# The row loads of the first eight down units move from the sync engine's queue to GpSimd's

## The chip, the cores and the metric

The kernel runs on one core of a Trainium2 chip. The metric is the time of one execution on the device in microseconds (us). The profile names the engines PE (TensorE, matmuls), PEld (TensorE, weight loads), DVE (VectorE), ACT (ScalarE), POOL (GpSimd) and SP (the sync engine, which here only issues transfers). "SPq" is SP's queue of transfers, and "POOLq" is POOL's.

## The reference

The reference is one decoder block on a sequence of 1024 tokens of width 1024, in float32. The part that this case is about is its last line, the channel mixer:

```python
xn2 = rmsnorm(x, norm2_g[l])
x = x + jnp.square(jax.nn.relu(xn2 @ w_up[l])) @ w_down[l]
```

Ahead of it stand dilated attention and retention, their gated merge and the output projection, which the change does not touch. `w_up` is 1024 x 4096 and `w_down` is 4096 x 1024. The first of the two products is called "up" here and the second "down".

## The kernel before

Every float32 factor is split into a high and a low half (`split`, L352 on ACT for the high half, L355 on DVE for the low), and a product is made of three matmuls: high by high, high by low, low by high. In tile names h and l mark the halves (`xh`, `xl`, `wh`, `wl`). The large products are done by a scheme of Strassen's kind: of each 2 x 2 block product, seven smaller products N1 to N7 are made, from sums of quarters, and their results are added or subtracted on DVE and ACT.

**Up.** There are 16 up units (j), each with seven products. Their left operands come from `w_up`, and their right operands are the seven pairs `OP7["N1"]` to `OP7["N7"]`, which hold sums of the normalised activations. ACT applies relu and square (L1222, L1223), DVE makes the sums for down (L1230), `split` writes a tile `hs`, and SP stores it to the DRAM buffer `h_d` (L1240). There are four `hs` tiles.

**Down.** There are 32 down units: u = 4c + t, where c is one of eight blocks of the inner dimension and t one of four blocks of tokens. A unit needs its rows of `h_d`, 7 products x 2 x 128 columns for 128 partitions: one transfer for the high half (`xh`) and one for the low (`xl`), 896 KB each. `load_rows(u)` issues both (L1256). The rows lie in three places in turn, which are the `OP7` pairs of N1, N5 and N3 once up no longer needs them. Each unit has seven products of six matmuls. `down(u, name)` makes one product: N1 is copied out of its bank by ACT with the sign turned (L1276) so that N6 and the later ones of that bank can add to it, and the other results go to the output sums `Y`, by an ACT copy when the sum begins (L1283) and by a DVE addition otherwise (L1285). The weights of down are loaded as raw quarters by SP (L208, `raw<-in_w_down`) into four buffers; DVE makes sums of them (L184), and `split` makes the pieces.

**Order.** PE's order is written out by hand. In the last up unit, `load_rows(0)` follows N1, `load_rows(1)` follows N5, `load_rows(2)` follows N3, and down's first two products are mixed in. After that each unit u goes:

```python
for name, later in (("N6", False), ("N5", False), ("N1", True), ("N7", False), ("N2", True),
                    ("N3", False), ("N4", False)):
    if u + later < len(units):
        down(u + later, name)
load_rows(u + 3)
```

So the rows of unit u+3 can be loaded when N4 of unit u is done, and they are first wanted by N1 of unit u+3, nine products later. The order on the other engines and on their transfer queues is made by a planner from its own costs, and each of them works through its order in sequence. An instruction that waits holds back what is behind it on its engine. POOL has short operations early in the kernel (powers for the norms, L369), and at the end it issues the 16 transfers that add `Y` to the output (L1287).

Of the kernel before, what the change touches and what calls it, by code (L numbers as in the profile page):

```python
# [10 lines left out]
F = mybir.dt.float32  # L11
# [290 lines left out]
def hybrid_block(ctx: ExitStack, tc: tile.TileContext, a: dict, out: bass.AP):  # L302
    nc = tc.nc
# [27 lines left out]
    h_d = dram.tile([FF // 512, 2, 4, P, 7, 2, P], F, name="h_d")  # L331
# [180 lines left out]
    with ExitStack() as ph:  # L512
# [96 lines left out]
        for n, t in enumerate(TILES):  # L609
# [4 lines left out]
            for k in range(KT):  # L614
                wh, wl = W[us[k // 2]]
                o = (k % 2) * 512
# [4 lines left out]
            c = px.tile([P, 512], F, name="c", bufs=1)  # L621
# [62 lines left out]
    for u in range(len(TOKEN)):  # L684
        n1, part = {}, {}
        for name in ("N1", "N2", "N6", "N5", "N3", "N7", "N4"):
            for t in range(4):
# [3 lines left out]
                for k in range(4):  # L691
                    wh, wl = W["att", u, name, k // 2]
                    o = (k % 2) * 512
# [7 lines left out]
                elif name == "N2":  # L701
                    c = cp.tile([P, 512], F, name="c")
# [7 lines left out]
                elif name == "N3":  # L710
                    c = cp.tile([P, 512], F, name="c")
# [306 lines left out]
    with ExitStack() as ph:  # L1018
# [56 lines left out]
        for d in range(KT):  # L1075
            ub, = W.take(1)
            for cs in halves():
                pp = project(0, d, cs, ub)
                t = pm2.tile([P, 512], F, name="s0")
# [31 lines left out]
    with ExitStack() as ph:  # L1111
# [41 lines left out]
        def load_rows(n):  # L1153

            nb, t = order[n]
            ts = slice(t * P, (t + 1) * P)
            xt = pn.tile([P, 512], F, name="xr")
            nc.sync.dma_start(xt, a["x"][ts, halves()[nb]])
            y0 = None
            if nb == 1:  # L1160
                y0 = pn.tile([P, 512], F, name="y0")
                nc.sync.dma_start(y0, out[ts, :512])
            ahead.append((xt, y0))

        load_rows(0)
        for nb in range(2):
            us = W.take(4)
            ns = halves()[nb]
            for n, t in enumerate([t for b, t in order if b == nb]):
                ts = slice(t * P, (t + 1) * P)  # L1170
                if len(ahead) < len(order):
                    load_rows(len(ahead))
                xt, y0 = ahead[NT * nb + n]
                pm = mm.tile([P, 512], F, name="mm")
                terms = []
                for k in range(KT):
                    wh, wl = W[us[k // 2]]
                    o = (k % 2) * 512
                    terms.append((*X(k, ts), wh[:, o:o + 512], wl[:, o:o + 512]))
                ends = {2 * i + 1: (lambda i=i, us=us: W.free(us[i])) for i in range(4)} if n == NT - 1 else None  # L1180
                pipe.step(pm, terms, ends)
                y = xt
                nc.vector.tensor_tensor(y, pm, xt, op=OP.add)
                nc.scalar.activation(pm, y, AF.Square, accum_out=ssq[:, t, nb:nb + 1])
                nc.sync.dma_start(out[ts, ns], y)
                if nb == 1:
                    nc.vector.tensor_tensor(ssq[:, t, 2:3], ssq[:, t, 0:1], ssq[:, t, 1:2], op=OP.add)
                    rsqrt(ssq[:, t, 3:4], ssq[:, t, 2:3], 1.0 / D)
                    xn = pn.tile([P, D], F, name="xn2")
                    for q, (cs, x2) in enumerate(zip(halves(), (y0, y))):  # L1190
                        nc.vector.scalar_tensor_tensor(xn[:, cs], x2, ssq[:, t, 3:4], g2[:, cs],
                                                       op0=OP.mult, op1=OP.mult)
                        pipe.at(2 if n > 5 else 1, lambda xn=xn, t=t, q=q: turn_xn(xn, t, q))
# [4 lines left out]
    with ExitStack() as ph:  # L1198
# [50 lines left out]
        def load_rows(u):  # L1249

            if u < len(units):
                c, t = units[u]
                rows[u] = []
                for i, x in enumerate(OP7[("N1", "N5", "N3")[u % 3]]):
                    x = x.rearrange("p a b -> p (a b)")[:, :7 * 2 * P]
                    nc.sync.dma_start(x.bitcast(F), h_d[c, i, t].rearrange("p o k q -> p (o k q)"))  # L1256
                    rows[u].append(x.rearrange("p (o k q) -> p o k q", o=7, k=2))

        def down(u, name):
# [31 lines left out]
        for j, name in strassen_order(NU):  # L1291
            product("up", j, name, unit, OP7, temps, result)
            if j == NU - 1:
                if name == "N1":
                    load_rows(0)
                if name == "N2":
                    parts = [x.rearrange("p a b -> p (a b)") for x in OP7[name]]
                    for i, part in enumerate("ab"):
                        W.places["n2" + part] = [x[:, 1024 * i:1024 * i + 1024] for x in parts]
                    W.free(("place", "n2"))  # L1300
                if name == "N5":
                    load_rows(1)
                if name == "N7":
                    down(0, "N1")
                if name == "N3":
                    load_rows(2)
                    down(0, "N2")
# [129 lines left out]
```

## Time and profile before

| what | value |
|---|---|
| median of 3 runs | 2247.35 us (2246.47 to 2249.44) |
| the profiled execution, its own time | 2249.58 us |
| its span in the profile | 2247.8 us |
| PE busy | 2189.5 us, 97% |
| DVE busy | 1433.9 us, 64% |
| ACT busy | 1108.9 us, 49% |
| POOL busy | 195.6 us, 9% |
| transfers | 392.77 MB, 175 GB/s on the mean |

The profile's page gives busy time by engine, a picture of the span in 40 slices, the chain of work that ended last, and groups of instructions. A busy PE is not a PE at its peak, since the ends of matmuls are modelled. A timeline row gives the start, the duration, the engine, the line and the operation with its output and inputs; in square brackets stands how long the engine was idle before it and what ended that. A row of waits gives the total, the number and the longest. A DMA share above 1 means that the transfer engines were full.

### The profile page before, as it was taken

The page shows a single profiled execution, that of the slowest core. Times are in us where ns is not written, and L with a number is a line of the kernel's source. Part 1 is how long each engine was busy: PE and PEld are TensorE (multiplying, and loading weights), DVE is VectorE, ACT ScalarE, POOL GpSimd, SP SyncE. Part 2 cuts the span into 40 slices and gives each one's busy share as a digit, 9 for nine tenths or more (in the row PEclk, how much of TensorE's full clock was granted, in tenths as well). Part 3 has the DMA queues.
Part 4 walks back from the last instruction along what each step waited for, and adds up shares of the span by engine and source line. Part 5 has one row for each costly group of instructions (what it writes and reads, how often), then busy time and mean ns, then how long its engine had stood idle before and what let it go on. Part 6 is the DMA issues. An engine that isn't in the chain of part 4 may idle for free.

```text
span 2247.8 us, 28538 instructions
## 1 busy us (share of the span) xinstructions
PE 2189.5 (97%) x10064; PEld 1797.2 (80%) x10064; DVE 1433.9 (64%) x2543; ACT 1108.9 (49%) x1936; POOL 195.6 (9%) x180
## 2 busy tenths in 40 slices
PE   8999999999999999989999999999899999899998
PEld 6788788888788887878888788888788888688887
DVE  6766675455555666647767852453878888776863
ACT  6433444467844567735555533122667777522210
POOL 3313553000000000000000000000000000000002
PEclk9999999999999999999999999999999999999999
DMA  6443443544545555454433494554378889966657
GB/s 194 131 132 113 131 112 114 158 143 145 171 148 168 161 157 165 129 180 130 124 108 101 139 295 154 169 180 143 99 215 248 248 248 287 316 248 244 246 222 173
DMA packets 346560, 392.77 MB, mean 175 GB/s; under 512 B 34738, under 2 KB 271922, under 8 KB 346163
## 3 DMA queue, kind: packets, MB, share of 16 engines
q1 hardware_dynamic: 344114, 386.77, 55.1%
q0 software_dynamic: 2304, 4.20, 1.3%
q8 instruction: 79, 1.29, 0.2%
q14 instruction: 63, 0.51, 0.1%
HBM read 252.39 MB, written 138.51 MB: 174 GB/s over the span
## 4 chain that ended last, share of the span: by engine, by line
PE 78%; DVE 6%; DMA 5%; ACT 5%; issue 3%; POOL 2%; SPq 0%; POOLq 0%; ACTq 0%; DVEq 0%
PE mm L255 45%; PE ms L255 27%; DVE wl L355 1%; PE tr L790 1%; PE tr L809 1%; ACT wh L352 1%; DMA xl<-h_d 1%; DVE xl L355 1%; PE tr L648 1%; DMA h_d<-hs 1%; POOL x L550 1%; PE ms L931 1%; DVE raw L151 1%; PE tr L802 1%; PE tr L987 1%
## 5 line engine op out<-in xcount | busy, mean ns | idle before, releaser
L355 DVE TENSOR_TENSOR wl<-raw,wh 128x1024 fp32r<-128x1024 f32 (+1 forms) x292 | 331.4, 1140 | 185.1 <-ACT wh L352 183.2
L352 ACT ACTIVATE wh<-raw 128x1024 fp32r<-128x1024 f32 (+1 forms) x292 | 287.3, 987 | 268.4 <-PE ms L255 125.4
L255 PE MATMUL mm<-xh,wh 128*128 128x512 f32 x896 | 347.3, 411 | 1.2 <-ACT wh L352 1.2
L255 PE MATMUL mm<-xl,wh 128*128 128x512 f32 x896 | 330.0, 392 | 1.7 <-DVE xl L355 1.7
L255 PE MATMUL mm<-xh,wl 128*128 128x512 f32 x768 | 301.9, 393 | 0.5 <-DVE wl L355 0.5
L255 PE MATMUL mm<-wh,xh 128*128 128x512 f32 x736 | 297.9, 405 | 2.5 <-ACT ms L1276 2.5
L255 PE MATMUL mm<-wh,xl 128*128 128x512 f32 x736 | 289.1, 393 | 2.4 <-DMA xl<-h_d 2.4
L255 PE MATMUL mm<-wl,xh 128*128 128x512 f32 x736 | 287.8, 391 | 0.0
L255 PE MATMUL ms<-xh,wh 128*128 128x512 f32 x544 | 226.2, 416 | 3.5 <-ACT u L427 1.6
L255 PE MATMUL ms<-xh,wl 128*128 128x512 f32 x544 | 213.1, 392 | 0.0
L255 PE MATMUL ms<-xl,wh 128*128 128x512 f32 x544 | 212.8, 391 | 0.0
L255 PEld LDWEIGHTS mm<-xh,wh 128*128 128x128 f32 x896 | 169.6, 189 | 33.3 <-ACT wh L352 1.6
L255 PEld LDWEIGHTS mm<-xl,wh 128*128 128x128 f32 x896 | 169.6, 189 | 31.9 <-DVE xl L355 2.1
L255 PEld LDWEIGHTS mm<-xh,wl 128*128 128x128 f32 x768 | 144.8, 189 | 32.3 <-DVE wl L355 1.0
L255 PEld LDWEIGHTS mm<-wh,xl 128*128 128x128 f32 x736 | 138.7, 188 | 33.7 <-DMA xl<-h_d 3.2
L255 PEld LDWEIGHTS mm<-wh,xh 128*128 128x128 f32 x736 | 139.4, 189 | 29.0 <-ACT ms L1276 3.3
L255 PEld LDWEIGHTS mm<-wl,xh 128*128 128x128 f32 x736 | 139.6, 190 | 25.9
L255 PE MATMUL ms<-wh,xh 128*128 128x512 f32 x336 | 138.3, 412 | 7.0 <-DVE c L703 4.7
L255 PE MATMUL ms<-wh,xl 128*128 128x512 f32 x336 | 133.7, 398 | 2.3 <-DVE xl L355 2.3
L255 PE MATMUL ms<-wl,xh 128*128 128x512 f32 x336 | 133.5, 397 | 0.8 <-DVE ss L368 0.8
L255 PEld LDWEIGHTS ms<-xh,wh 128*128 128x128 f32 x544 | 102.7, 189 | 24.4 <-ACT u L427 2.4
L255 PEld LDWEIGHTS ms<-xh,wl 128*128 128x128 f32 x544 | 102.3, 188 | 22.0
(282 smaller groups left out, 3818.8 us busy)
## 6 DMA issues: line engine op xcount, KB each, us to landing
h_d<-hs SPq DMA_DIRECT2D x112, 512.0 KB, 4.3
xh<-h_d SPq DMA_DIRECT2D x32, 896.0 KB, 5.1
xl<-h_d SPq DMA_DIRECT2D x32, 896.0 KB, 6.9
raw<-in_w_att_q SPq DMA_DIRECT2D x48, 512.0 KB, 4.3
raw<-in_w_up SPq DMA_DIRECT2D x32, 512.0 KB, 3.8
raw<-in_w_down SPq DMA_DIRECT2D x32, 512.0 KB, 5.0
qk_d<-T SPq DMA_DIRECT2D x48, 256.0 KB, 3.5
raw<-in_w_gate_q SPq DMA_DIRECT2D x16, 512.0 KB, 4.3
```

Of the source, the lines that this page charges most:

```text
L151: self.nc.vector.tensor_tensor(x, x, y, op=OP.add)
L255: self.nc.tensor.matmul(ps, x, y, start=start, stop=stop, skip_group_check=not first)
L352: hi = nc.scalar.activation(dst_h, src, AF.Copy)
L355: nc.vector.tensor_tensor(dst_l, src, dst_h.bitcast(F), op=OP.subtract)
L550: nc.gpsimd.tensor_tensor(x[v], x[v], x[u], op=op)
L648: nc.tensor.transpose(pt[:, i, :], c[:, i * P:(i + 1) * P], ident)
L790: nc.tensor.matmul(sp[:, :w], q[:, e * P:(e + 1) * P], k[:, k0 * P:k0 * P + w], start=True, stop=True)
L802: nc.tensor.transpose(tb[:, j * P:(j + 1) * P], st["p"][:, j * P:(j + 1) * P], ident)
L809: nc.tensor.matmul(po[:, :DH], st["t"][:, j * P:(j + 1) * P], v[:, k0 + j, :], start=(j == 0), stop=(j == nk - 1))
L931: nc.tensor.matmul(sp[:, :P], kT[:, f], qT[:, f], start=(f == 0), stop=(f == 1))
L987: nc.tensor.transpose(pt[:, f, :], it["o"][:, f * P:(f + 1) * P], ident)
```

## The change

The transfers of `load_rows(u)` for u from 0 to 7 are issued by GpSimd, and those of the other 24 units by SP as before. Addresses, sizes and tiles are the same.

```diff
                 rows[u] = []
                 for i, x in enumerate(OP7[("N1", "N5", "N3")[u % 3]]):
                     x = x.rearrange("p a b -> p (a b)")[:, :7 * 2 * P]
-                    nc.sync.dma_start(x.bitcast(F), h_d[c, i, t].rearrange("p o k q -> p (o k q)"))
+                    (nc.gpsimd if u < 8 else nc.sync).dma_start(x.bitcast(F), h_d[c, i, t].rearrange("p o k q -> p (o k q)"))
                     rows[u].append(x.rearrange("p (o k q) -> p o k q", o=7, k=2))
```

## The prediction

> **What bounds the kernel now.** I read the page's busy shares first (below, first row), then a table of stages, then PE's waits in the stage that the edit touches, then the timelines of PE, SP, ACT, DVE and POOL there. The stage table, with PE's busy time after the stage's length, and the granted clock, the DMA share and GB/s at the end of a row:
>
> ```profile
> PE 2189.5 (97%) x10064; PEld 1797.2 (80%) x10064; DVE 1433.9 (64%) x2543; ACT 1108.9 (49%) x1936; POOL 195.6 (9%) x180
> ...
> core 0: us, PE busy (x) PEld busy (x) DVE busy (x) ACT busy (x) POOL busy (x), PEclk, DMA share, GB/s
> 1920.00:1940.00 20.00, 17.02 (x74) 13.47 (x73) 12.45 (x17) 12.62 (x21) 0.00 (x0) 1.00 1.06 335
> 1940.00:1960.00 20.00, 17.37 (x68) 13.52 (x68) 14.39 (x15) 10.92 (x14) 0.00 (x0) 0.91 0.80 303
> 1960.00:1980.00 20.00, 16.75 (x67) 13.15 (x65) 14.43 (x15) 9.31 (x12) 0.00 (x0) 0.91 0.72 268
> 2000.00:2040.00 40.00, 40.00 (x177) 32.95 (x176) 29.86 (x38) 10.23 (x12) 0.00 (x0) 1.00 0.64 238
> ```
>
> From 2000 on PE has no gap, so what PE gains or loses before that moves the end by as much. The holes lie between 1920 and 1980, where up gives way to down. The waits of PE between 1870 and 2060, and the one row of SP's that goes with them (total, times, longest):
>
> ```profile
> PE mm L255 <- DMA xl<-h_d: 5.7, 3, 3.2
> PE mm L255 <- ACT ms L1276: 2.6, 3, 2.2
> SPq L1256 <- PE ms L255: 50.9, 12, 8.9
> ```
>
> Three waits for the low half (xl) of a down unit's rows, all in the first units; the SP queue itself stands 50.9 us behind row loads that wait for PE. PE's timeline shows what the three cost. The first row is from the chain that ended last: 12 matmuls in 2.72 us, so 0.227 us from one to the next and 1.36 us for a product of six.
>
> ```profile
> 1983.38 2.72 PE ms L255 x12
> 1936.67 0.39 PE L255 MATMUL mm<-wl,xh 128*128 128x512 f32 x1
> 1939.03 0.50 PE L255 MATMUL mm<-wh,xl 128*128 128x512 f32 x1 [1.98 <-DMA xl<-h_d]
> 1940.30 0.52 PE L255 MATMUL ms<-xl,xh 128*128 128x512 f32 x1
> 1943.94 0.39 PE L255 MATMUL mm<-wl,xh 128*128 128x512 f32 x1
> 1950.07 0.39 PE L255 MATMUL mm<-wl,xh 128*128 128x512 f32 x1
> 1950.89 0.50 PE L255 MATMUL mm<-wh,xl 128*128 128x512 f32 x1 [0.43 <-DMA xl<-h_d]
> 1955.66 0.50 PE L255 MATMUL mm<-wh,xh 128*128 128x512 f32 x1 [2.21 <-ACT ms L1276]
> 1962.82 0.39 PE L255 MATMUL mm<-y1al,xh 128*128 128x512 f32 x1
> 1966.45 0.50 PE L255 MATMUL mm<-y1ah,xl 128*128 128x512 f32 x1 [3.25 <-DMA xl<-h_d]
> 1967.71 0.60 PE L255 MATMUL ms<-xl,xh 128*128 128x512 f32 x1
> 1971.36 0.39 PE L255 MATMUL mm<-y1bl,xh 128*128 128x512 f32 x1
> ```
>
> Counting products in PE's fixed order, the three waits are the first product (N1) of units 2, 3 and 4. Between 1940.30 and 1943.94 nine matmuls take 3.64 us where nine take 2.04 (9 x 0.227), and 3.65 from 1967.71 to 1971.36: after the two long waits the clock is low for a while, which the stage table shows as 0.91. Now SP's queue over the same time (an "x3" merges issues; the waits for their inputs lie inside; the last row is from the list of issues, with the median us to landing):
>
> ```profile
> 1923.79 1.07 SPq L1256 DMA_DIRECT2D xh<-h_d  x1
> 1927.84 3.75 SPq L1240 DMA_DIRECT2D h_d<-hs  x3
> 1931.64 0.76 SPq L1256 DMA_DIRECT2D xl<-h_d  x1
> 1934.98 4.89 SPq L208 DMA_DIRECT2D raw<-in_w_down  x3
> 1939.97 0.38 SPq L1256 DMA_DIRECT2D xh<-h_d  x1
> 1947.09 0.32 SPq L1256 DMA_DIRECT2D xh<-h_d  x1
> 1954.04 5.43 SPq L208 DMA_DIRECT2D raw<-in_w_down  x4
> 1959.57 0.38 SPq L1256 DMA_DIRECT2D xl<-h_d  x1
> ...
> raw<-in_w_down SPq DMA_DIRECT2D x32, 512.0 KB, 5.0
> ```
>
> Unit 2's xh goes out at 1923.79, its xl, free at the same moment, 7.9 us later, behind three stores that wait for DVE. Unit 4's xh goes at 1947.09, its xl at 1959.57, 12.5 us later, behind four weight loads that wait for a raw buffer. Unit 3's pair (1939.97) stands behind three weight loads. The lateness comes from the order on one queue, not from the rows.
>
> **The change, part by part.** Sixteen issues (two for each of units 0 to 7) leave SP and join POOL; bytes and tiles stay.
>
> What POOL pays. POOL's neighbours in time: its last instruction before, and its next, with a direct case of its issue cost, then how long transfers take (KB each, median us from issue to landing; the last row is the range of all row loads):
>
> ```profile
> 1608.82 0.54 POOL L369 TENSOR_TENSOR ssq<-ssq,half 128x1 f32<-128x1 f32 x1 [8.15 <-DVE ssq L368]
> 2202.92 1.06 POOL L1287 DMA_DIRECT2D out<-Y  x1 [593.55 <-DVE Y L1285]
> 2225.70 0.88 POOL L1287 DMA_DIRECT2D out<-Y  x1 [0.29 <-DVE Y L1285]
> out<-Y POOLq DMA_DIRECT2D x16, 256.0 KB, 5.1
> xl<-h_d SPq DMA_DIRECT2D x32, 896.0 KB, 6.9
> DMA to landing us min/median/max: 4.4/6.3/10.4
> ```
>
> POOL is idle for 593.55 us around the stage, so the loads pass nothing there, and the final out transfers come 200 us later. No row shows POOL issuing a row load. Below: SP's 0.32 us. Above: POOL's 1.06 us for 256 KB scaled by bytes to 896 KB, 3.7 us. I take 1.06, POOL's own dearest issue, since both transfers are 128 partition rows. Landing may differ on another queue too: 4.4 to 10.4 us is what the rows gave behind SP; I take 6.9.
>
> What a unit has in hand. A row buffer becomes free after N4 of unit u-3; nine products (N6, N5, N1, N7, N2, N3, N4, N6, N5) and two matmuls later PE wants xl: 9 x 1.36 + 2 x 0.23 = 12.7 us. For unit 2 it is 1923.79 to 1936.90, 13.1 us. POOL needs 2 x 1.06 + 6.9 = 9.0 us, and 12.5 with the longest landing. So units 2 to 4 should be in time, and units 5 to 7, in time already, pay 1 to 2 us of a slack of about 4. Units 0 and 1 are wanted long after their issue: nothing.
>
> What comes off PE's path. Unit 2: 1936.67 to 1939.03 less one step, 2.13, and the low clock 3.64 - 2.04 = 1.60: 3.73 us. Unit 3: 1950.07 to 1950.89 less a step: 0.59. Unit 4: 1962.82 to 1966.45 less a step, 3.40, and 3.65 - 2.04 = 1.61: 5.01. Together 9.33 us.
>
> What is late next. At 1955.66 PE waits for ACT: N2 of unit 3 needs ACT's copy of N1's bank, and that copy stands in ACT's queue behind a weight split that waits for DVE, which waits for PE earlier on:
>
> ```profile
> 1954.06 1.06 ACT L352 ACTIVATE w1bh<-raw 128x1024 fp32r<-128x1024 f32 x1 [1.53 <-DVE raw L184]
> 1955.03 0.58 ACT L1276 ACTIVATE ms<-mm 128x512 f32<-128x512 f32 x1
> 1952.76 1.22 DVE L184 TENSOR_TENSOR raw<-raw,raw 128x1024 f32<-128x1024 f32 x1
> 1945.96 0.69 DVE L1285 TENSOR_TENSOR Y<-Y,mm 128x512 f32<-128x512 f32 x1 [2.64 <-PE mm L255]
> ```
>
> DVE's run of work starts from a product of PE at 1945.96, so it moves up with unit 2's 3.73 us; unit 3's 0.59 lies behind that start, so this wait only grows by 0.59. Net: 9.33 - 0.59 = 8.74 us.
>
> What SP gains. Its stores and weight loads no longer stand behind row loads; the weight loads still wait for DVE, and the stores feed units far later. I cost it at nothing. The cover is DVE; were it gone, the row loads left on SP (unit 8 on) would be next to show it.
>
> The sum: the profiled execution took 2249.58 us (span 2247.8), which is 2.2 above the median of the runs, 2247.35. 2249.58 - 8.74 = 2240.8 for such an execution, 2238.6 for the median.
>
> [...] The rows say that a gap of 2.4 us (unit 2) brought the low clock, while the 2.4 us gap ending at 1955.66 did not. [...]
>
> **The rivals.**
> ACT takes over. If DVE's run of weight work is held not by PE but by the weight loads landing (issued from 1934.98 to 1939.87, 5.0 us more to landing), ACT's copy stays at 1955.03, PE waits there for all that units 2 and 3 gave, and a low clock follows (1.6). Left is 5.01 - 1.6 = 3.4: 2243.9. Against it: the landings end near 1944.9, just before DVE would ask.
>
> The engines are full. The DMA share is 1.06 in 1920:1940, so rows issued sooner might land no sooner: 2247.35. Against it: unit 4's 12.5 us is a queue's, at a share of 0.72 to 0.80. [...]
>
> Slower: POOL's issue is dear. If one issue takes e and the landing L, PE waits once 2e + L passes 12.7 us. At e = 3.7 and L = 10.4 it is 17.8, 5.1 late. A stall at one unit lengthens the next one's time in hand, so every second unit stalls (2, 4, 6): 3 x (5.1 + 1.6) = 20.1 against 9.33 lost now: 2258. It is a loss from 2e + L = 14.2 on (three stalls of 1.5 + 1.6). For it: DVE is busy 12 to 14 of 20 us here, and POOL might have to wait for it. Against: 0.88 and 1.06 with DVE running. [...] No run here shows a row load on POOL.
>
> The wait for ACT goes too. All engines but PE follow a planner's order; if the copy comes ahead of the split, another 0.59 and 2.37 us (2.6 less a step) go: 8.74 + 2.96 = 11.7: 2235.6.
>
> **How the numbers follow.** Forecast 0.60; ACT takes over 0.12; engines full 0.07; POOL dear 0.14; the ACT wait goes as well 0.07. The forecast's own range is 2236 to 2241.5. To leave out no more than 0.2 the range goes from 2235 to 2249: the dear POOL and part of the best case lie outside. 0.2% is 4.5 us, about what a measurement of this kernel tells from no change. Faster: 0.60 + 0.07 and a quarter of the ACT case (without the low clock it is 2242.3), 0.70. Same: the rest of it and the full engines, 0.16. Slower: 0.14.
>
> **What would show it.** Right: sixteen row loads on POOL at about 1 us each, xh and xl of a unit next to each other; no wait of PE for xl<-h_d in units 2 to 4; the granted clock back at 1.00 where it was 0.91; a wait for ACT of 2.4 to 3 us left. Wrong: POOL issues of 3 us or more, a wait for xl at units 5 to 7, or ACT's copy no sooner than now. A new order on ACT or DVE would make the sum wrong in either direction.

## The result, and the profile after

The changed kernel takes 2253.32 us (median of 10 runs, 2250.42 to 2256.64), and the kernel before took 2246.56 us beside it (10 runs). The ratio is 1.0038, with a 95% interval of 1.0028 to 1.0048. So the change makes the kernel slower by 0.38%, some 8.5 us by the ratio; the forecast was a gain of 8.74 us.

The row loads came in time, as forecast, and PE still lost more. The stage table of the kernel after has the columns of the one in the prediction. Its first two rows are of the last up unit; the second block has the same two stretches of the kernel before.

```profile
core 0: us, PE busy (x) PEld busy (x) DVE busy (x) ACT busy (x) POOL busy (x), PEclk, DMA share, GB/s
1880.00:1900.00 20.00, 17.43 (x71) 13.99 (x70) 14.34 (x20) 11.84 (x19) 1.34 (x2) 0.91 1.02 315
1900.00:1920.00 20.00, 20.00 (x90) 16.57 (x89) 16.87 (x22) 15.02 (x25) 2.14 (x4) 1.00 0.81 254
1920.00:1940.00 20.00, 9.51 (x36) 7.41 (x35) 14.05 (x17) 10.86 (x18) 0.00 (x0) 0.74 1.08 373
1940.00:1960.00 20.00, 16.73 (x67) 13.31 (x67) 9.53 (x11) 8.63 (x13) 2.17 (x4) 0.91 0.69 243
1960.00:1980.00 20.00, 20.00 (x90) 16.57 (x89) 14.36 (x16) 10.43 (x14) 2.16 (x4) 1.00 0.58 225
```

```profile
1880.00:1900.00 20.00, 20.00 (x90) 16.54 (x89) 18.14 (x26) 15.43 (x25) 0.00 (x0) 1.00 1.04 300
1900.00:1920.00 20.00, 18.75 (x82) 14.90 (x81) 16.24 (x21) 14.17 (x23) 0.00 (x0) 1.00 1.02 308
```

From 1960 to 1980 PE is now full, where it had 16.75 us. But 1920 to 1940 fell from 17.02 to 9.51 us, and 1880 to 1900 from 20.00 to 17.43. In both stretches the DMA share is above 1. It was above 1 in the kernel before too, all the way from 1880 to 1940 (1.04, 1.02 and 1.06), so what the change altered is not how full the engines were but which transfers they carried at a time. PE's waits after, from 1870 to 2060 (total, times, longest):

```profile
PE ms L255 <- ACT Y L1283: 10.5, 1, 10.5
PE ms L255 <- DVE Y L1285: 3.3, 1, 3.3
PE mm L255 <- ACT u L430: 2.6, 1, 2.6
PE mm L255 <- ACT ms L1276: 0.2, 1, 0.2
```

No wait for xl is left. In its place PE waits 10.5 us, once, for ACT's copy into the output sum `Y`. What held ACT is in ACT's own waits over that time, and in the landing times of the `hs` stores from 1860 to 1960; the two rows of before come first, then those of after.

```profile
ACT hs L352 <- DMA h_d<-hs: 3.5, 4, 1.0
DMA to landing us min/median/max: 3.3/5.3/9.2
```

```profile
ACT hs L352 <- DMA h_d<-hs: 13.6, 4, 5.8
DMA to landing us min/median/max: 3.2/5.7/13.8
```

ACT may write an `hs` tile again only when its old store has landed. The longest store went from 9.2 to 13.8 us, and ACT's wait from 3.5 to 13.6 (four waits each). The timeline of ACT after shows how that reaches the `Y` copy:

```profile
1926.18 0.63 ACT L352 ACTIVATE hs<-u 128x512 fp32r<-128x512 f32 x1 [2.59 <-DMA h_d<-hs]
1930.27 0.63 ACT L352 ACTIVATE hs<-q 128x512 fp32r<-128x512 f32 x1 [3.46 <-DMA h_d<-hs]
1930.80 0.58 ACT L1222 ACTIVATE q<-ms 128x512 f32<-128x512 f32 x1
1931.28 1.05 ACT L352 ACTIVATE y1ah<-raw 128x1024 fp32r<-128x1024 f32 x1
...
1932.91 1.06 ACT L352 ACTIVATE y1ch<-raw 128x1024 fp32r<-128x1024 f32 x1
1933.88 0.62 ACT L352 ACTIVATE hs<-q 128x512 fp32r<-128x512 f32 x1
1934.40 0.58 ACT L1283 ACTIVATE Y<-ms 128x512 f32<-128x512 f32 x1
```

PE starts again at 1935.03, when the copy at 1934.40 ends. Before, the same copy ran at 1927.51, right behind relu and square, and two of the `hs` splits and both weight splits that now stand ahead of it came after it:

```profile
1926.00 0.58 ACT L1222 ACTIVATE q<-ms 128x512 f32<-128x512 f32 x1
...
1927.51 0.58 ACT L1283 ACTIVATE Y<-ms 128x512 f32<-128x512 f32 x1
```

So two things happened: transfers that ACT waits for became late, and the planner gave ACT, DVE and the stores and weight loads of SP another order, in which more work that waits stands ahead of what PE needs. PE's own order is unchanged.

**The measure used below.** The time from launch to this stage varies: at its start the kernel after stood 4.9 us ahead, and a second profile of the kernel before, unchanged, stood 3.4 us ahead of its first (1885.01 and 1888.38). So besides the whole time I use a stage: from ACT's copy of N1 in the last up unit (L422) to SP's issue of xh of the last down unit. Before, then after:

```profile
1888.38 0.58 ACT L422 ACTIVATE ms<-mm 128x512 f32<-128x512 f32 x1
2213.90 0.32 SPq L1256 DMA_DIRECT2D xh<-h_d  x1
```

```profile
1883.49 0.58 ACT L422 ACTIVATE ms<-mm 128x512 f32<-128x512 f32 x1
2215.12 0.32 SPq L1256 DMA_DIRECT2D xh<-h_d  x1
```

That is 325.5 us before and 331.6 after, 6.1 longer. PE's waits in the window add up to 10.3 us before (2.6, 5.7 and twice 1.0, in ACT's copies) and 16.6 after, 6.3 more. A second profile of each kernel, on another chip, gave 322.5 before and 335.2 after, with a longest `hs` store of 7.9 and 15.8 us and waits of ACT for stores of 4.9 and 16.5. So one stage time repeats to 3 or 4 us, and a single difference smaller than that is not read as an effect; the lengthened stores repeat.

### The profile page after: what moved, and what is told of

Same layout as the page of the kernel before. It is cut to its first block, busy times and chain, and to the rows that moved or that the text cites. A ratio compares the mean times of both kernels' runs of the same rounds, so it can differ in the third digit from the quotient of the medians.

```text
span 2248.6 us, 28549 instructions
## 1 busy us (share of the span) xinstructions
PE 2183.0 (97%) x10064; PEld 1793.2 (80%) x10064; DVE 1433.5 (64%) x2543; ACT 1109.9 (49%) x1936; POOL 202.0 (9%) x196
## 4 chain that ended last, share of the span: by engine, by line
PE 79%; DVE 6%; ACT 4%; DMA 4%; issue 3%; POOL 3%; SPq 0%; POOLq 0%; ACTq 0%; DVEq 0%
PE mm L255 45%; PE ms L255 28%; DVE wl L355 1%; PE tr L790 1%; PE tr L809 1%; ACT wh L352 1%; DMA h_d<-hs 1%; POOL x L550 1%; PE tr L648 1%; DVE xl L355 1%; DMA raw<-in_w_att_q 1%; DMA raw<-in_w_down 1%; PE ms L931 1%; PE tr L802 1%; PE tr L987 1%
## 5 line engine op out<-in xcount | busy, mean ns | idle before, releaser
L255 PE MATMUL mm<-xl,wh 128*128 128x512 f32 x896 | 329.4, 391 | 1.7 <-DVE xl L355 1.7
L255 PE MATMUL ms<-wh,xh 128*128 128x512 f32 x336 | 137.8, 410 | 10.1 <-DVE c L703 4.5
```

Source lines behind the costliest of these rows:

```text
L255: self.nc.tensor.matmul(ps, x, y, start=start, stop=stop, skip_group_check=not first)
```

## The experiments

**How an order was held.** Where a kernel is to keep a given order on ACT, DVE or SP, edges that only fix the order of issue were added at the end of the function. `ORDER` lists the instructions of down's first units on each engine.

```diff
+    for names in ORDER:
+        for first, then in zip(names, names[1:]):
+            tc.add_manual_dep(held_in["I-%d" % then], "I-%d" % first, NoSync)
```

"Old order" below is the order of the kernel before, "new order" that of the kernel after. The list for SP begins behind the two row loads of unit 0, so where these stand on SP is left to the planner.

### The two parts apart

`order_kept` has all rows of units 0 to 7 on POOL, and ACT, DVE and SP hold the old order.

```diff
+ORDER = [old order of ACT, of DVE, of SP without the row loads of units 0 to 7]
```

> The changed kernel (row loads of units 0 to 7 on POOL), with ACT, DVE and the rest of SP's queue held in the order that they have in the kernel before. Theory 'order' (the loss comes from the new order that the planner gave ACT and DVE): the waits for rows go and nothing new comes, about 2238 us, 9 below before, with a wait of PE for the ACT copy of 2 to 3 us left. Theory 'transfers' (row loads on a second queue slow the stores of hs, so ACT waits for hs tiles in any order): 2250 us or more, with ACT waiting 10 us or more in total for h_d<-hs between 1870 and 1960, against 3.5 before.

`order_alone` has all rows on SP, and ACT and DVE hold the new order; SP's queue is left to the planner here, which ordered it anew.

```diff
-(nc.gpsimd if u < 8 else nc.sync).dma_start(...)
+nc.sync.dma_start(...)
+ORDER = [new order of ACT, of DVE]
```

> The kernel before (all row loads on SP), with ACT and DVE held in the order that they have in the changed kernel. 'Order': the loss comes without POOL, 2253 us or more, with a wait of PE for an ACT copy of Y of about 10 us. 'Transfers': the loss stays away, 2244 to 2250 us, and ACT waits no more than 5 us for h_d<-hs.

Measured: `order_kept` 2249.86 us, ratio 1.0016 (1.0003 to 1.0029), stage 328.4. `order_alone` 2259.85 us, ratio 1.0067 (1.0054 to 1.0079), stage 338.5. Waits of PE, ACT's longest on a transfer and the landing of the `hs` stores, in `order_kept`, then in `order_alone`:

```profile
PE mm L255 <- ACT ms L1276: 5.1, 2, 4.9
PE ms L255 <- ACT Y L1283: 4.0, 2, 2.9
PE mm L255 <- ACT u L430: 2.4, 1, 2.4
ACT hs L352 <- DMA h_d<-hs: 9.4, 3, 5.7
ACT y1bh L352 <- DMA raw<-in_w_down: 3.3, 1, 3.3
DMA to landing us min/median/max: 3.3/5.4/13.7
```

```profile
PE ms L255 <- ACT Y L1283: 14.5, 1, 14.5
ACT y1ch L352 <- DMA raw<-in_w_down: 9.9, 1, 9.9
DMA to landing us min/median/max: 3.2/5.4/7.5
```

Neither part alone gains, and each run came out close to what the explanation by its own part had forecast (2250 us or more, and 2253 or more). With the old order the wait for xl is still gone, and ACT waits for stores (9.4 us) and for the weights. With the rows on SP the longest store lands in 7.5 us, and ACT waits for none between 1860 and 1960: so the long stores come with the rows on POOL and not with the new order. The new order without POOL puts a weight split, whose load is 9.9 us late in SP's new queue order, ahead of the same `Y` copy. Counted from the stage's start, that copy ran at 39.1 us before (1927.51 - 1888.38), at 43.4 in `order_kept`, at 50.9 after (1934.40 - 1883.49) and at 57.3 in `order_alone`. So at this copy the rows' move costs 4.2 us and the new order (of ACT, DVE and SP) 7.6 more. The second profiles of the three kernels put the copy at 38.0, 40.2 and 52.4 us: 2.2 and 12.2. The larger part of the 10.5 us that PE waits for this copy belongs to the order.

### Which units pay

`late_units`: rows on POOL for units 3 to 7 only, old order. `late_free`: the same with the planner free. `unit0_sp`: units 1 to 7, old order.

```diff
-(nc.gpsimd if u < 8 else nc.sync).dma_start(...)
+(nc.gpsimd if 3 <= u < 8 else nc.sync).dma_start(...)   # late_units, late_free
+(nc.gpsimd if 1 <= u < 8 else nc.sync).dma_start(...)   # unit0_sp
```

> Only the row loads of units 3 to 7 on POOL, those of 0 to 2 on SP, with ACT, DVE and SP held in the order of the kernel before. Both theories: unit 2's wait (3.7 us with its low clock) stays, those of units 3 and 4 go (0.6 and 5.0): 2241 to 2243 us. 'Order' has it above order_kept by about 3.7 us, 'transfers' has it well below order_kept, since hardly a store is left when POOL's first load goes out.

> Only the row loads of units 3 to 7 on POOL, and the planner free to order everything else. 'Order': anything from 2241 us (the old order nearly kept) to above 2250, as its new order has it, and a difference to late_units comes from ACT or DVE work standing elsewhere. 'Transfers': the same as late_units, 2241 to 2243 us.

> Row loads of units 1 to 7 on POOL, unit 0's on SP as before; ACT, DVE and SP in the order of the kernel before. 'Stage' is the time from ACT's copy for the last up unit's N1 (L422) to the issue of the last down unit's xh: 325.5 us before, 331.6 in the changed kernel, 328.4 with the order kept. Theory 'transfers': unit 0's two loads, issued 30 us ahead of need while stores fill the engines, hold back stores of hs and so cost the wait for ACT's L430 (2.4 and a low clock of about 1.4): stage about 324.6, and that wait is gone. Rival 'later loads' (the loads of units 1 and 2 do it as well): the hs waits of 5 us or more stay and the stage stays at 328.

Measured: 0.9998 (0.9989 to 1.0007), stage 324.4, for `late_units`; 0.9997 (0.9987 to 1.0008), stage 324.4, for `late_free`; 1.0005 (0.9995 to 1.0015), stage 325.5, for `unit0_sp`. All are the kernel before within what can be told; for `late_units` both explanations had forecast a gain. `unit0_sp` has no wait for L430, the copy in the last up unit on which PE waited 2.6 us after the change. In the kernel after, the split right ahead of that copy waited for its store:

```profile
1893.08 0.63 ACT L352 ACTIVATE hs<-q 128x512 fp32r<-128x512 f32 x1 [5.78 <-DMA h_d<-hs]
```

In `unit0_sp` the same split waits 2.94 us, so unit 0's rows on POOL made PE's wait. In `late_units` PE waits 5.3 us for ACT's copies of N1 and 2.4 for an xl, and the planner left free does no harm when only late units move.

### Moving the copies

If a late `Y` copy costs 10.5 us, it should help to put it first. `copies_first` is the kernel after with that done (and N7's addition on DVE put ahead of weight splits); `unit0_sp_moves`, `late_ms_first` and `units_4_7_ms` do the like for ACT's copy of N1 of unit 3 (L1276).

```diff
 ORDER of ACT:
-  hs split, hs split, relu, ..., Y copy of N6(0), Y copy of N5(0)
+  relu, Y copy of N6(0), Y copy of N5(0), hs split, hs split, ...      # copies_first, after's order otherwise
-  three weight splits, copy of N1(3)
+  copy of N1(3), three weight splits      # unit0_sp_moves (with Y of N6(0) first), late_ms_first, units_4_7_ms
```

> The changed kernel with its own order, but for three instructions of ACT (relu of the last up result, and the copies of N6 and N5 of unit 0 to Y) moved ahead of the two hs splits that wait for stores, and one of DVE (Y of unit 0's N7) moved ahead of the weight splits. 'Order': the waits of 10.5 us for ACT's Y and 3.3 for DVE's Y go or shrink to 2, with their low clock; stage 331.6 - 10 to 14, that is 318 to 322. 'Transfers': the stores still hold ACT, the same time is lost one product later, stage 328 to 332.

> As unit0_sp, with ACT's copy for N1 of unit 3 (L1276) moved ahead of three weight splits, and the copy of N6 of unit 0 to Y moved ahead of two hs splits. 'Order': the waits for ACT's ms (4.9 with the order kept) and Y (2.9) go or shrink to under 1, and the stage is 316 to 319 us, the whole 7 to 9 below before. 'Transfers': the weight splits were late since their loads were, so the wait moves on to a product that needs w1; stage 322 or more.

> As late_units (units 3 to 7 on POOL, old order, stage 324.4), with ACT's copy for N1 of unit 3 moved ahead of three weight splits. 'Order': the wait of 4.9 us for that copy and its low clock of 1.4 go, stage 318 to 319.5. 'Transfers': the wait shows up at a later product, stage 323 or more.

> Only the loads of units 4 to 7 on POOL (their first goes out when the stores are over), the old order, and ACT's copy for N1 of unit 3 ahead of three weight splits, as in late_ms_first (323.4). 'Transfers': unit 3's rows no longer compete with the weight loads ahead of y1bh; unit 2's wait stays, unit 4's 5.0 and the copy's 2.4 go: stage 318 to 319.5. 'Order': as late_ms_first, 323 to 324.

Measured: `copies_first` 1.0019 (1.001 to 1.0028), stage 328.2; `unit0_sp_moves` (units 1 to 7 on POOL) 0.9999 (0.999 to 1.0009), 325.5; `late_ms_first` (units 3 to 7) 1.0001 (0.999 to 1.0012), 323.4; `units_4_7_ms` (units 4 to 7) 0.9998 (0.9988 to 1.0007), 322.6. None reached the stage that the order alone as a cause would have given in the first three (316 to 322), and the fourth missed the 318 to 319.5 expected of fewer competing transfers. The first took away the wait it aimed at, and another took its place. PE's main waits of `copies_first`, then of `late_ms_first`:

```profile
PE mm L255 <- ACT ms L1276: 10.4, 2, 10.2
PE mm L255 <- ACT u L430: 3.0, 1, 3.0
```

```profile
PE ms L255 <- DVE Y L1285: 5.6, 1, 5.6
PE ms L255 <- ACT Y L1283: 3.0, 2, 2.0
```

In the second the copy of N1 runs early, and then ACT stands 4.8 us for weights of down that have not landed, and DVE's additions wait for their turn behind it. A place in an order does not bring what a transfer brings. Two more tries put the weight work behind the sums. `late_reordered` is `late_ms_first` with two weight splits on ACT and N7's additions on DVE changed over; `late_xl` moves only the xl of unit 2 and the rows of units 4 to 7, with the copy of N1(3) and the addition of N7(2) ahead.

```diff
 ORDER:
-  ACT: y1b split, y1c split, copies   DVE: weight sums, addition of N7(2)
+  ACT: copies, y1b split, y1c split   DVE: addition of N7(2), weight sums      # late_reordered
-(nc.gpsimd if u < 8 else nc.sync)
+(nc.gpsimd if 4 <= u < 8 or (u, i) == (2, 1) else nc.sync)                     # late_xl
```

> As late_ms_first (units 3 to 7 on POOL, 323.4), with the splits y1b and y1c on ACT moved behind the copies that PE waits for, and DVE's additions to Y put between its weight work. 'Order': the waits of 5.6 for DVE's Y and 2.0 for ACT's Y go; stage 317 to 319. 'Transfers': the weight loads still land late, so the wait moves to the products that need w1b and y1b: 321 to 323.

> POOL takes only xl of unit 2 and the loads of units 4 to 7; ACT's copy for N1 of unit 3 is ahead of three weight splits, DVE's addition for N7 of unit 2 ahead of two of its weight steps, the rest in the old order. Against units_4_7_ms (stage 322.6), which kept waits of 2.1 and 1.7 for xl and of 2.7 for DVE's Y: if unit 2's xl can go early at the cost of one store only, stage 317 to 320 and the median about 2240; 'transfers': xl ahead of three stores brings an ACT wait for hs of some 3 us more, stage 321 to 323.

Both are slower: 1.0012 (1.0003 to 1.0021), stage 329.4, with one wait of 8.6 us for a copy of N1; and 1.0036 (1.0023 to 1.0048), stage 331.6, with waits of 8.5 us for ACT's copies of N1, 3.6 for xl and 2.4 for xh. `moves_sp` makes the last one's two moves in the kernel before, with every row on SP:

```diff
 ORDER of ACT and DVE, all rows on SP:
-  ..., copy of N1(3)     ..., addition of N7(2)
+  copy of N1(3), ...     addition of N7(2), ...
```

> The kernel before, all row loads on SP, with only the two moves of late_xl on ACT and DVE. It tells what of late_xl comes from the order and not from POOL: the wait of 2.2 for ACT's ms goes, unit 4's wait for xl grows by as much, since xl then waits for weight loads as before: stage 324.5 to 326.

Measured 1.0026 (1.0015 to 1.0037), stage 328.0. PE waits twice for xl, 7.4 us the longer time:

```profile
PE mm L255 <- DMA xl<-h_d: 10.9, 2, 7.4
```

In every move that was tried, what was brought forward made something else late, with the rows on either queue.

### Fewer bytes

What was missing was a run that separates the order of a queue from the volume in it. Three kernels load only half of each partition's row for units 0 to 3 (that half of the rows is left out of the computation's input); the instructions stay. `half_rows` has the rows on POOL and the new order, `half_rows_kept` POOL and the old order, `half_rows_sp` SP and the old order.

```diff
-.dma_start(x.bitcast(F), src)
+.dma_start(x.bitcast(F)[:, :896 if u < 4 else 1792], src[:, :896 if u < 4 else 1792])
```

> The changed kernel with its own order of ACT and DVE held, and the row loads of units 0 to 3 cut to half of each partition's row (the other half is left out, and the products use what lies in the buffer). 3.6 MB less to move between 1880 and 1945, some 11 us of the engines at 335 GB/s. Theory 'transfers' (the engines are full there, so rows that come sooner make stores and weight loads come later): the waits of ACT for h_d<-hs fall from 13.6 us to under 6, and the stage from 331.6 to 322 to 326. Rival 'order' (the order of ACT and DVE costs by itself): 329 to 332.

> As order_kept (all eight units on POOL, old order of ACT, DVE and SP, stage 328.4), with the row loads of units 0 to 3 cut to half of each partition's row in the same way. 'Transfers': ACT's waits for hs (9.4) and for the weight load ahead of y1bh (3.3) nearly go, PE's waits of 2.4, 2.9 and 4.9 shrink to the 2.2 of before or less; stage 316 to 320, what the prediction had. 'Order': no change from 328 to 326.

> The kernel before (row loads on SP, its order of ACT, DVE and SP held) with the row loads of units 0 to 3 cut to half of each partition's row. A control for half_rows_kept (stage 318.4, all eight units on POOL). If the 10 us that half_rows_kept gained over order_kept come from room on the engines that the move to POOL needs ('transfers'), the kernel before gains little from the same cut, since its rows wait on SP's order: unit 4's wait of 5.0 stays, units 2 and 3 get at most their shorter landing; stage 321 to 325. If fewer bytes alone give the gain, the stage is 315 to 319 here too.

| rows of units 0 to 3 | queue, order | ratio | stage |
|---|---|---|---|
| whole | SP, old (before) | 1 | 325.5, again 322.5 |
| whole | POOL, old (`order_kept`) | 1.0016 (1.0003 to 1.0029) | 328.4, again 326.6 |
| whole | POOL, new (after) | 1.0038 (1.0028 to 1.0048) | 331.6, again 335.2 |
| half | SP, old | 0.9979 (0.9968 to 0.9989) | 316.9 |
| half | POOL, old | 0.9957 (0.9944 to 0.9969) | 318.4 |
| half | POOL, new | 1.0017 (1.0007 to 1.0027) | 327.3 |

With half the bytes the stage falls by 7.1 us on SP (from the mean, 324.0) and by 9.1 on POOL with the old order (from 327.5). On POOL with the old order, nothing but the bytes differs from `order_kept`: the longest `hs` store falls from 13.7 to 8.0 us, and ACT's waits for stores from 9.4 to 4.2. In the new order (`half_rows`) they fall from 13.6 to 5.3, but PE's wait for the `Y` copy only from 10.5 to 9.0, so that wait does not hang on the stores alone. The two rows are of `half_rows_kept` and of `half_rows`:

```profile
ACT hs L352 <- DMA h_d<-hs: 4.2, 3, 1.7
...
PE ms L255 <- ACT Y L1283: 9.0, 1, 9.0
```

The SP kernel is the control, and it gains nearly as much, where 321 to 325 was expected if only the move needed the room. So most of the gain with half the bytes does not need the move. One thing besides the bytes differs from the kernel before: unit 0's xl went out ahead of three stores that it had stood behind. PE's waits in it, the start of its stage, its SP rows for unit 4, and PE's wait for that unit's xl:

```profile
PE mm L255 <- ACT ms L1276: 2.8, 2, 2.6
PE mm L255 <- DMA xl<-h_d: 1.6, 2, 1.3
```

```profile
1881.78 0.58 ACT L422 ACTIVATE ms<-mm 128x512 f32<-128x512 f32 x1
...
1933.66 0.32 SPq L1256 DMA_DIRECT2D xh<-h_d  x1
1940.98 5.43 SPq L208 DMA_DIRECT2D raw<-in_w_down  x4
1946.50 0.38 SPq L1256 DMA_DIRECT2D xl<-h_d  x1
...
1952.92 0.50 PE L255 MATMUL mm<-y1ah,xl 128*128 128x512 f32 x1 [1.32 <-DMA xl<-h_d]
```

Unit 4's rows are whole here too, and its xl still goes out 12.8 us behind its xh, past the same four weight loads (12.5 before). But it goes out 64.7 us after the stage's start (1946.50 - 1881.78), where it was 71.2 before (1959.57 - 1888.38), and PE waits 1.32 us for it, where it waited 3.25. All waits for xl fell from 5.7 to 1.6. So most of the lateness went with the bytes while the order of the queue from unit 1 on stayed; for units 2 and 3 the late rows are themselves half as large. The longest `hs` store lands in 6.7 us here. The new order still costs with half the rows: 327.3 against 318.4.

`before_2`, `after_2` and `order_kept_2` are the three kernels again, unchanged, one run each on another chip, to see how far a stage time repeats.

```diff
 (no edit)
```

> The kernel before once more, for how well the stage (ACT's copy for the last up unit's N1 to the issue of the last unit's xh) repeats: 325.5 in the first profile. If it repeats within 1 us, the differences of 3 and more between the kernels stand; if it moves by 3, those between before, order_kept and unit0_sp do not.

> The changed kernel once more: stage 331.6 in the first profile, with waits of PE of 10.5 for ACT's Y, 3.3 for DVE's Y and 2.6 for ACT's L430. The same waits within 1 us, if they come from the order and from transfers that compete every time.

> order_kept once more: stage 328.4 in the first profile, with waits for ACT of 2.4 (L430), 2.9 (Y) and 4.9 (ms). If POOL's loads cost by themselves, the stage stays 2 to 4 above before's.

The stages were 322.5, 335.2 and 326.6 us. In the means of two profiles, after stands 9.4 us above before and order_kept 3.5. The second profile of after shows the same wait, 11.8 us for the `Y` copy.

## Why the prediction was wrong

**What POOL pays: right, and cheaper.** POOL's rows after, and the queue's two rows with the median landing:

```profile
1880.91 0.78 POOL L1256 DMA_DIRECT2D xl<-h_d  x1 [274.98 <-DMA raw<-in_w_down]
1909.65 0.55 POOL L1256 DMA_DIRECT2D xl<-h_d  x1 [27.40 <-PE mm L255]
1916.45 0.54 POOL L1256 DMA_DIRECT2D xl<-h_d  x1 [5.73 <-PE mm L255]
...
xl<-h_d POOLq DMA_DIRECT2D x8, 896.0 KB, 7.0
xh<-h_d POOLq DMA_DIRECT2D x8, 896.0 KB, 6.4
```

An issue took 0.54 us on the median (0.78 the first; I took 1.06), and landing 6.4 to 7.0 (I took 6.9). The rival in which POOL is dear falls. Nor did a busy DVE hold POOL up here: from 1909 to 1911 and from 1916 to 1918 DVE is busy without a gap, and POOL's four issues there took 0.54 or 0.55 us; from 1957 to 1959 DVE does nothing, and the two issues there took 0.54.

**What comes off PE's path: right.** All three waits for xl went, and the granted clock from 1960 to 1980 is 1.00, where it was 0.91.

**"I cost it at nothing": this step failed.** The prediction let SP's stores and weight loads go unpriced, since "the stores feed units far later". The rows of a store do; the store's *tile* does not. There are four `hs` tiles, and ACT's next split waits for the oldest store (13.6 us in four waits after). Row loads from a second queue ran beside the stores in stretches where the DMA share was 1.02 and 1.08, the longest store went from 9.2 to 13.8 us, and ACT's wait grew by 10.1 us. ACT's copies for PE stand behind that in one queue. In `order_kept`, with ACT's order as before, PE's waits add up to 11.5 us, against 10.3 before (second profiles: 11.5 and 7.2): what the rows gave was given back. `half_rows_kept` and `order_alone` tie the long stores to the rows' bytes on POOL.

**"Units 0 and 1 ... nothing": failed for unit 0.** Its rows, issued at 1880.91, some 30 us ahead of their need, took transfer time from the last up unit. PE waited 2.6 us for L430, behind an `hs` split that waited 5.78 us for its store; in `unit0_sp` that split waits 2.94, and PE's wait is gone.

**"The lateness comes from the order on one queue, not from the rows": failed in its second half.** The queue's order does make the rows late: on POOL, with all their bytes, they come in time (`order_kept` has no wait for xl). But `half_rows_sp` keeps that order from unit 1 on and loses most of the lateness with the bytes (1.6 us of waits for xl, 5.7 before), so the two act together. The rival of full engines, which I gave 0.07, was nearest, but not as I wrote it: the rows did land sooner (no wait for xl is left), and other transfers landed later (the longest store in 13.8 us, 9.2 before). My argument against it, unit 4's 12.5 us between two issues at a share of 0.72 to 0.80, looked at the wrong stretch and at the wrong distance: the 12.5 us are still there (12.8) in the run with half the bytes, which has little of the wait. My reading, argued from these rows and not tested by itself, is that what counts is how far everything had come by then, and that this was set ahead of 1940, at a share of 1.02 to 1.06 before. No variant with whole rows on a second queue came out ahead by more than its interval: the lowest ratio of them is 0.9997 (0.9987 to 1.0008), of `late_free`.

**The order on ACT and DVE: named, not priced; this failed as well.** The prediction said that a new order "would make the sum wrong in either direction", and gave a number only to the lucky one. It costs 3 us of stage by the first profiles (331.6 against 328.4), which alone is within the scatter, 5.9 by the means of two, and 8.9 with half the rows. The whole times agree: 1.0016 with the old order, 1.0038 with the new.

**What is late next: the place right, the size not.** ACT's copy of N1 of unit 3 was to make PE wait 3.0 us. In `order_kept` it is 4.9, and ACT's weight splits ahead of it wait for loads that landed later (3.3 us at y1bh). That is close to the rival in which ACT takes over, to which I gave 0.12.

**The clock.** The wait at N2 of unit 3, whose growth to 3.0 us the prediction expected, is gone after (0.2 us are left of the waits for L1276). Another gap brought the low clock after, that of 2.57 us in the last up unit:

```profile
1894.25 0.79 PE L255 MATMUL mm<-xh,wh 128*128 128x512 f32 x1 [2.57 <-ACT u L430]
```

Its first matmul took 0.79 us, and the granted clock was 0.50 from 1894.20 to 1897.30; the 0.91 of the first row of the table is the mean of 20 us. Before, the clock was 0.54 from 1940.20 to 1943.90, behind unit 2's gap of 1.98 us, and 1.00 from 1955.60 to 1958.00, behind the gap of 2.21. The shorter of those two gaps was followed by the low clock and the longer was not, so these rows give no length of gap from which the clock falls.

**What stays open.** Whether the rows on POOL cost by themselves when the order is held: +3.5 us of stage is within the scatter, and the ratio's interval begins at 1.0003. With half rows, the stage puts SP ahead by 1.5 us and the whole time puts POOL ahead by 0.2%, on different chips; that is not settled. No kernel with all of the computation came out faster than before beyond its interval.

## What to carry to other kernels

In this stage, with a DMA share of 1.02 to 1.06 from 1880 to 1940 in the kernel before, loads that were moved to another queue to go out sooner only changed which transfer was late: PE's waits for xl went from 5.7 us to none, and ACT's for stores from 3.5 to 13.6. Where the share is as high, list the stores and loads that are in flight beside it, and which tiles they hold. A store is awaited by whoever writes its tile next, here ACT, and not only by whoever reads its data. Where a planner orders the other engines, a change of one queue reorders them too: hold the old order once, to tell the two effects apart.

## What the runs showed of the hardware that was not expected

POOL issued a load of 896 KB in 0.54 us on the median, less than the 0.86 to 1.06 us of its accumulating transfers of 256 KB before, and in `half_rows_kept` the xh loads of its first six units, four of them of 448 KB, took 0.54 to 0.58: in these runs the issue did not go by bytes. With the row loads on a second queue the slowest of the `hs` stores took half as long again (13.8 us against 9.2), and twice as long in the second profiles (15.8 against 7.9), while their median moved only from 5.3 to 5.7 (5.6 to 5.7), so a median of landing times would have hidden it.
